# Attention layer of a hybrid decoder trunk: low parts of the weights and steps of the rotation move from GpSimd to VectorE

## The chip, the cores and the metric

The kernel runs on one core of a Trainium2 chip. A core has five engines with a queue of their own each: TensorE (PE in the profile, its weight loads PEld), VectorE (DVE), ScalarE (ACT), GpSimd (POOL) and SyncE (SP), which here issues all DMAs. Each engine takes its instructions in order and waits on semaphores for what others make. The metric is the device time of one execution in microseconds; less is better.

## The reference, cut to what matters

Two layers on a sequence of 1024 tokens with 1024 features: an attention layer with low-rank queries and keys (MLA), then a recurrent layer (RWKV-7). Each layer also attends to a memory of 256 tokens, gates with SiLU, and projects back. Only the first layer is touched by the change.

```
h = rmsnorm(x, norm_g[i]);  m = rmsnorm(mem, mem_norm_g[i])
mem_k, mem_v = split_cols(m @ w_mem_kv[i], (X_WIDTH, X_WIDTH))
u = h @ w_in_mla[j]
c_q, c_kv, k_rope_raw, q_mem, gate = split_cols(u, (384, 256, 64, 512, 2048))
q  = (rmsnorm(c_q, q_norm_g) @ w_uq).reshape(B, S, 12, 128 + 64)     # the last 64 rotated
kv = (rmsnorm(c_kv, kv_norm_g) @ w_ukv).reshape(B, S, 12, 128 + 128)
mix = causal softmax attention of 12 heads (block of 128 queries at a time)
mem_out = memory_attention(q_mem, mem_k, mem_v)
x = x + concatenate([mix, mem_out]) * silu(gate) @ w_out[i]

def apply_rope(x, cos, sin):
    x1, x2 = x[..., 0::2], x[..., 1::2]
    return stack([x1 * cos - x2 * sin, x1 * sin + x2 * cos])
```

## The kernel before

All matrices are kept transposed: features on the 128 partitions, 512 tokens (half of the sequence, `hf` 0 or 1) along the row. A float32 product is made of three matmuls in a narrower type: every operand is split into a high part, rounded (`wh`, `xh`), and a low part, the rest (`wl`, `xl`); `mm3` (lines 162 to 164) multiplies high by high, high by low and low by high. A high part is a cast on ScalarE, a low part a subtraction.

`weights` (line 142) fetches a block of weights in pieces of 512 columns: a DMA into one of four raw buffers `wr`, the cast on ScalarE (line 153), the subtraction (line 155). Four buffers each for `wh` and `wl` mean that a piece can be split only when PE has done with the one four pieces earlier. Which engine subtracts is decided in line 154: VectorE in the recurrent layer (`self.lows` is set there, line 941), GpSimd in the attention layer, and the two in turn for the memory's weights (`shared`).

The attention layer (`layer0`, line 414) runs in this order.

- `load_x` and `low` (about the first 100 us): the two halves of x are loaded and split (lines 440 and 441), and six column blocks of 128 are projected for either half (`mm_331` to `mm_986`, eight products of three matmuls each).
- The norms. `squares` (lines 182 to 186) squares on ScalarE and adds up on VectorE (`sqa`); `rstd_rows` sums over the partitions with a tiny matmul (line 208), then makes the reciprocal root in twelve small VectorE steps (lines 194 to 210) and spreads it (line 213); `rstd_spread` turns it with four transposes on PE (line 220). Five such chains stand in this stretch: x's first half (`b_289`, `b_309`), its second half (`b_581`, `b_601`), the two low-rank norms (`b_717`, `b_737` and `b_804`, `b_824`) and the memory (`b_1045`, `b_1063`). `tables` (lines 493 to 514) makes the rotation's sine and cosine, one half of the tokens at a time.
- `mem_load`, `mem_norm`, `mem_kv`: the memory is normed in four steps (`mn` line 255, `mh` and `ml` lines 128 and 129) and multiplied with the memory's weights (`mm_1271`, `mm_1309` and on).
- `mem_heads` and `gates`: the memory's attention and the gates, until about 450 us.
- `attend` and `project` (about 450 to 890 us): 48 tasks, 12 heads by four blocks of 256 queries, with the scores two tasks ahead of the values; in between `project` makes queries, keys and values of the head two further on. Every second head also makes the rotated queries of two heads: `rope` (line 516) multiplies by the cosine on VectorE (522), the swapped halves by the sine on GpSimd (523), and adds; lines 640 and 641 subtract for their low parts on GpSimd. GpSimd also clears two blocks of the transposed probabilities a task (line 730).
- `out_proj` of the first half, to about 965 us; that of the second half runs under the recurrent layer, with `self.lows` set.

No order is written out by hand between the engines. The generators interleave the pieces as the program is written, and a scheduler then orders the instructions of each engine from its own estimates of when what is ready; buffers are given out in the same pass. So where an instruction goes to another engine, the order on the others moves with it.

Of the kernel before, what the change touches and what calls it, by code (L numbers as in the profile page):

```python
# [13 lines left out]
F32 = mybir.dt.float32  # L14
# [57 lines left out]
class Build:  # L72
    def __init__(self, tc, A, st):
        self.tc, self.nc, self.A = tc, tc.nc, A
        self.n, self.lows = 0, False
        pool = lambda name, bufs, **kw: st.enter_context(tc.tile_pool(name=name, bufs=bufs, **kw))
        self.const = pool("const", 1)
        self.wp = pool("w", 4)
        self.w2p = pool("w2", 1)
        self.ws = pool("ws", 4)  # L80
        self.smp = pool("sm", 4)
        self.heap = pool("heap", 54)
        self.heap2 = pool("heap2", 12)
        self.mmp = pool("mmp", 2, space=PSUM)
        self.dram = pool("dram", 1, space=DRAM)
        self.ysp = [None, None]
        dt = lambda s: self.dram.tile([P, T], F32, tag=s, name=s)
        self.mkd = [[dt(f"mk{l}{i}") for i in range(2)] for l in range(2)]
        self.mvd = [[dt(f"mv{l}{i}") for i in range(2)] for l in range(2)]
        self.carry = [self.dram.tile([P, P], F32, tag=f"cr{p}", name=f"cr{p}") for p in range(NH)]  # L90
        self.setup()
# [47 lines left out]
        self.split(hi[:], lo[:], src)  # L139
        return hi, lo  # L140

    def weights(self, src, cols=1024, shared=False):


        nc = self.nc
        res = []
        for c in range(0, cols, T):
            n = min(T, cols - c)
            raw = self.wp.tile([P, T], F32, tag="wr", name=self.name("wr"))
            hi = self.ws.tile([P, T], F32R, tag="wh", name=self.name("wh"))  # L150
            lo = self.ws.tile([P, T], F32R, tag="wl", name=self.name("wl"))
            nc.sync.dma_start(raw[:, :n], src[:, c : c + n])
            nc.scalar.copy(hi[:, :n], raw[:, :n])  # L153
            sub = nc.vector.tensor_sub if self.lows or shared and len(res) % 2 else nc.gpsimd.tensor_sub
            sub(lo[:, :n], raw[:, :n], hi[:, :n].bitcast(F32))  # L155
            res.append((hi, lo))
        return res

# [104 lines left out]
    def mem_kv(self, l, ms):  # L263

        nc, A = self.nc, self.A
        mk, mv = [], []
        for h in range(4):
            if h % 2 == 0:
                mk.append(self.g([P, 2, 256], s="mk"))
            w = self.weights(A["wmk"][l, h], shared=True)  # L270
            ps = self.mmt()
            self.gemm(ps[:, :256], w, ms, 8)
            nc.scalar.copy(mk[-1][:, h % 2, :], ps[:, :256])
        for cb in range(2):
            ws = self.weights(A["wmv"][l, cb, 0], shared=True) + self.weights(A["wmv"][l, cb, 1], shared=True)
            ps = self.mmt()
            for mb in range(2):
                for k in range(8):
                    hi, lo = ws[k // 2]
                    o = (k % 2) * 256  # L280
                    m = tuple(x[:, mb * P : mb * P + P] for x in ms[k])
                    self.mm3(
                        ps[:, mb * 256 : mb * 256 + 256], m, (hi[:, o : o + 256], lo[:, o : o + 256]), k == 0, k == 7
                    )
            t = self.g(s="mv")
            nc.scalar.copy(t[:], ps[:])
            mv.append(t)
        for i, t in enumerate(mk):
            nc.sync.dma_start(self.mkd[l][i][:].rearrange("p (h m) -> p h m", h=2), t[:])
        for i, t in enumerate(mv):  # L290
            nc.sync.dma_start(self.mvd[l][i][:], t[:])
# [122 lines left out]
    def layer0(self, ahead):  # L414

        nc, A, tc = self.nc, self.A, self.tc
        with ExitStack() as st:
# [46 lines left out]
            raw = [[None] * 6 for _ in range(2)]  # L464
# [27 lines left out]
            cos, sin = tl([P, S], F32, "cos"), tl([P, S], F32, "sin")  # L492
# [23 lines left out]
            def rope(q, hf):  # L516

                sl = slice(hf * T, hf * T + T)
                sw, t = self.g(s="rs"), self.g(s="rt")
                for b in range(4):  # L520
                    nc.sync.dma_start(sw[32 * b : 32 * b + 32, :], q[32 * (b ^ 1) : 32 * (b ^ 1) + 32, :])
                nc.vector.tensor_mul(t[:], q[:], cos[:, sl])
                nc.gpsimd.tensor_mul(sw[:], sw[:], sin[:, sl])
                nc.vector.tensor_add(t[:], t[:], sw[:])
                return t

# [7 lines left out]
            def lows(hf):  # L534
                cq.append(lora(0, 3, PQG, hf, lambda s: tl([P, T], F32R, s)))
                yield
                ckv.append(lora(3, 2, PKVG, hf, lambda s: self.g(dt=F32R, s=s)))
                yield
                kr.append((tl([P, T], F32R, f"krh{hf}"), self.g(dt=F32R, s="krl")))
                self.split(kr[hf][0][:], kr[hf][1][:], rope(raw[hf][5], hf)[:])  # L540
                yield
# [66 lines left out]
            def project(h):  # L608
# [3 lines left out]
                if h % 2 == 0:  # L612
                    w = self.weights(A["wuq"][12 + hp], 384)
                    hd["qr"], heads[h + 1]["qr"] = [], []
                    for hf in range(2):
                        ps = self.mmt()
                        self.gemm(ps[:], w, cq[hf], 3)
                        q = self.g(s="rq")
                        nc.scalar.activation(q[:], ps[:], AF.Copy, scale=ATT_SCALE)
                        rot.append(rope(q, hf))  # L620
                        yield
                hd["qn"], hd["kn"] = [], []
                w = self.weights(A["wuq"][h], 384)
# [5 lines left out]
                w = self.weights(A["wkn"][h], 256)  # L629
# [5 lines left out]
                for t in rot:  # L635

                    a, b = self.g(dt=F32R, s="qsa"), self.g(dt=F32R, s="qsb")
                    nc.scalar.copy(a[0:64, :], t[0:64, :])
                    nc.scalar.copy(b[64:128, :], t[64:128, :])
                    nc.gpsimd.tensor_sub(a[64:128, :], t[0:64, :], a[0:64, :].bitcast(F32))  # L640
                    nc.gpsimd.tensor_sub(b[0:64, :], t[64:128, :], b[64:128, :].bitcast(F32))
                    hd["qr"].append(a)
                    heads[h + 1]["qr"].append(b)
                if h % 2 == 0:

                    w = self.weights(A["wv"][hp], 512)[0]
# [114 lines left out]
            for _ in project(0):  # L761
                pass
            for _ in project(1):
                pass
# [14 lines left out]
    def layer1(self, x1, first, second):  # L779

        nc, A, tc = self.nc, self.A, self.tc
        with ExitStack() as st:
# [155 lines left out]
                    next(gen, None)  # L938
                    yield

            self.lows = True
            N, now = 2 * NH, [0]
            stages = [(project, ST[0]), (lambda i: self.prep(items[i], env), ST[1]), (lambda i: self.invert(items[i], env), ST[2]), (scan, ST[3]), (norm, ST[4])]
            extra = {}
# [434 lines left out]
```

## Time and profile before

| | |
|---|---|
| median of 3 runs | 2541.62 us (2540.92 to 2550.03) |
| the profiled execution | 2544.33 us, its span 2542.6 us |
| TensorE busy | 2434.1 us, 96% |
| VectorE busy | 1883.6 us, 74% |
| ScalarE busy | 1371.9 us, 54% |
| GpSimd busy | 285.0 us, 11% |
| mean granted TensorE clock | 0.991 |

Most of GpSimd's time lies in the attention layer: 186.3 us for 148 weight subtractions. TensorE is the busiest engine in all stages but the first 128 us, so a stall of it is time lost and a stall of another engine usually is not. A wait is read at the instruction that waits, with its releaser behind the arrow.

### The profile page before, as it was taken

Reading aid. Unit: us, or ns where it says so; the run is one execution under the profiler, and the core shown is the slowest. Engines: PE = TensorE matmul, PEld = TensorE weight load, DVE = VectorE, ACT = ScalarE, POOL = GpSimd, SP = SyncE. Lnnn points to the kernel's source line nnn. Section 1 sums busy time; section 2 is a strip of 40 time slices with the busy share of each in tenths; the row PEclk is TensorE's granted clock in tenths of the full one; section 3 lists DMA queues with packets and bytes.
Section 4 is the critical chain, followed back from the end, with each engine's and each line's share of the span. In section 5 each row is a group of like instructions: output and inputs, shape, how many; then the busy total and the mean of one; then the engine's idle time right before and its main releaser. Section 6 shows DMA issues by size and latency. Waiting matters only on the chain.

```text
span 2542.6 us, 39928 instructions
## 1 busy us (share of the span) xinstructions
PE 2434.1 (96%) x13298; PEld 2003.9 (79%) x13298; DVE 1883.6 (74%) x5564; ACT 1371.9 (54%) x2971; POOL 285.0 (11%) x344
## 2 busy tenths in 40 slices
PE   7899999999999999999999999999999999999997
PEld 5688777888888787878777777877787777788885
DVE  6655433677777647679888888788888888786986
ACT  5444335555445434556566665666666665654542
POOL 3332222322222240000000000000000000000000
PEclk8899999999999999999999999999999999999998
DMA  4242222111111345331222222322222223232341
GB/s 155 88 157 96 91 83 80 50 50 60 55 54 56 135 140 178 122 106 61 80 67 70 74 83 82 120 76 76 69 78 74 75 80 102 92 105 97 115 141 69
DMA packets 165983, 231.46 MB, mean 91 GB/s; under 512 B 46096, under 2 KB 67984, under 8 KB 165776
## 3 DMA queue, kind: packets, MB, share of 16 engines
q1 hardware_dynamic: 165776, 228.90, 27.5%
q8 instruction: 105, 1.72, 0.3%
q14 instruction: 102, 0.84, 0.1%
HBM read 187.66 MB, written 37.49 MB: 89 GB/s over the span
## 4 chain that ended last, share of the span: by engine, by line
PE 69%; DVE 16%; ACT 6%; issue 3%; DMA 2%; SPq 0%; DVEq 0%; POOL 0%; ACTq 0%; POOLq 0%
PE mm L162 14%; PE mm L163 13%; PE mm L164 13%; PE a L1088 3%; DVE tmp L1139 2%; PE c L1221 2%; PE pt L726 2%; DVE U L1143 2%; PE c L1224 1%; PE po L162 1%; PE y L1228 1%; PE po L163 1%; DVE wl L155 1%; PE y L1227 1%; PE po L164 1%
## 5 line engine op out<-in xcount | busy, mean ns | idle before, releaser
L153 ACT CAST wh<-wr 128x512 fp32r<-128x512 f32 (+3 forms) x500 | 298.6, 599 | 461.6 <-PE mm L163 363.0
L162 PE MATMUL mm<-xnh,wh 128*128 128x512 f32 x912 | 374.1, 411 | 0.8 <-DVE qml L134 0.6
L163 PE MATMUL mm<-xnl,wh 128*128 128x512 f32 x912 | 371.4, 407 | 0.0
L164 PE MATMUL mm<-xnh,wl 128*128 128x512 f32 x912 | 369.8, 406 | 0.0
L155 DVE TENSOR_TENSOR wl<-wr,wh 128x512 fp32r<-128x512 f32 (+2 forms) x352 | 237.2, 676 | 98.7 <-ACT wh L153 79.8
L155 POOL TENSOR_TENSOR wl<-wr,wh 128x512 fp32r<-128x512 f32 (+1 forms) x148 | 186.3, 1263 | 579.4 <-ACT wh L153 446.0
L162 PE MATMUL mm<-yh,wh 128*128 128x512 f32 x492 | 199.8, 406 | 5.5 <-DVE xr L391 5.3
L164 PE MATMUL mm<-yh,wl 128*128 128x512 f32 x492 | 197.6, 402 | 0.0
L162 PEld LDWEIGHTS mm<-xnh,wh 128*128 128x128 f32 x912 | 172.2, 189 | 30.4 <-issue 2.6
L163 PE MATMUL mm<-yl,wh 128*128 128x512 f32 x492 | 196.1, 399 | 0.0
L163 PEld LDWEIGHTS mm<-xnl,wh 128*128 128x128 f32 x912 | 172.4, 189 | 27.2 <-issue 1.4
L164 PEld LDWEIGHTS mm<-xnh,wl 128*128 128x128 f32 x912 | 172.2, 189 | 27.2 <-issue 1.0
L1069 POOL MEMSET SAV<- 64x512 f32 x48 | 24.9, 524 | 1385.6 <-DVE m L1261 250.7
L162 PE MATMUL mm<-xh,wh 128*128 128x512 f32 x416 | 168.9, 406 | 7.2 <-ACT xh L440 7.2
L163 PE MATMUL mm<-xl,wh 128*128 128x512 f32 x416 | 168.6, 405 | 2.9 <-DVE xl L441 2.9
L164 PE MATMUL mm<-xh,wl 128*128 128x512 f32 x416 | 168.1, 404 | 0.0
L1139 DVE TENSOR_TENSOR tmp<-As,U 128x60 f32<-128x60 f32 (+24 forms) x744 | 156.8, 211 | 13.2 <-DMA U<-in_cst_dram 1.1
L1143 DVE TENSOR_TENSOR U<-U,tmp 128x60 f32<-128x60 f32 (+24 forms) x744 | 157.2, 211 | 11.9
L1235 ACT ACTIVATE sc<-S,f 128x128 f32<-128x128 f32 x168 | 67.4, 401 | 170.0 <-DVE S L1236 155.5
L304 ACT ACTIVATE p<-b,sm 128x512 f32<-128x512 f32 (+2 forms) x144 | 82.9, 579 | 117.2 <-DVE sm L301 78.0
L391 DVE TENSOR_TENSOR xr<-mm,xr 128x512 f32<-128x512 f32 x123 | 84.5, 689 | 77.7 <-PE mm L164 77.2
L162 PEld LDWEIGHTS mm<-yh,wh 128*128 128x128 f32 x492 | 93.1, 189 | 24.3 <-DVE xr L391 3.5
(362 smaller groups left out, 6214.3 us busy)
## 6 DMA issues: line engine op xcount, KB each, us to landing
wr<-in_wu_dram SPq DMA_DIRECT2D x292, 256.0 KB, 2.6
wr<-in_wo_dram SPq DMA_DIRECT2D x122, 256.0 KB, 2.6
yr<-y SPq DMA_DIRECT2D x60, 256.0 KB, 3.7
As<-sysd SPq DMA_DIRECT2D x24, 512.0 KB, 4.3
y<-y SPq DMA_DIRECT2D x32, 256.0 KB, 2.0
y<-sg SPq DMA_DIRECT2D x32, 256.0 KB, 2.0
g<-u SPq DMA_DIRECT2D x24, 256.0 KB, 2.4
gt<-g SPq DMA_DIRECT2D x24, 256.0 KB, 2.8
```

The source lines that it names most:

```text
L153: nc.scalar.copy(hi[:, :n], raw[:, :n])
L155: sub(lo[:, :n], raw[:, :n], hi[:, :n].bitcast(F32))
L162: mm(ps, a[0], b[0], start=start, stop=False)
L163: mm(ps, a[0], b[1], start=False, stop=False)
L164: mm(ps, a[1], b[0], start=False, stop=stop)
L304: nc.scalar.activation(p[:, :own], ps[:, :own], AF.Exp, bias=sm[:, 0:1], accum_out=sm[:, 2 + i : 3 + i])
L391: nc.vector.tensor_add(xs[m][:], ps[:], xs[m][:])
L726: nc.tensor.transpose(pt[:, o : o + P], src, self.ident)
L1088: mm(ps[:, j * 256 : j * 256 + 256], BK[c // 4][:, c % 4, :], AR[:, c, :], start=True, stop=True)
L1139: E.tensor_tensor(out=tmp[:, 0:u, 0:n], in0=As[:, 0:u, u : u + 1].broadcast_to([P, u, n]), in1=U[:, u : u + 1, i0:8].broadcast_to([P, u, n ...
L1143: E.tensor_tensor(out=U[:, 0:u, i0:8], in0=U[:, 0:u, i0:8], in1=tmp[:, 0:u, 0:n], op=ALU.add)
L1235: ACT.activation(sc[:], cur, AF.Copy, scale=fc)
```

## The change

Line 154 goes: every low part of a weight is subtracted on VectorE. In `rope` the product with the sine, and in `project` the two subtractions of the rotated queries' low parts, go to VectorE too. The argument `shared` and the switch `self.lows` go with it. What is computed is the same. GpSimd keeps its clearing of buffers and the mask.

```diff
-    def weights(self, src, cols=1024, shared=False):
+    def weights(self, src, cols=1024):
...
             nc.scalar.copy(hi[:, :n], raw[:, :n])
-            sub = nc.vector.tensor_sub if self.lows or shared and len(res) % 2 else nc.gpsimd.tensor_sub
-            sub(lo[:, :n], raw[:, :n], hi[:, :n].bitcast(F32))
+            nc.vector.tensor_sub(lo[:, :n], raw[:, :n], hi[:, :n].bitcast(F32))
...
                 nc.vector.tensor_mul(t[:], q[:], cos[:, sl])
-                nc.gpsimd.tensor_mul(sw[:], sw[:], sin[:, sl])
+                nc.vector.tensor_mul(sw[:], sw[:], sin[:, sl])
                 nc.vector.tensor_add(t[:], t[:], sw[:])
...
                     nc.scalar.copy(b[64:128, :], t[64:128, :])
-                    nc.gpsimd.tensor_sub(a[64:128, :], t[0:64, :], a[0:64, :].bitcast(F32))
-                    nc.gpsimd.tensor_sub(b[0:64, :], t[64:128, :], b[64:128, :].bitcast(F32))
+                    nc.vector.tensor_sub(a[64:128, :], t[0:64, :], a[0:64, :].bitcast(F32))
+                    nc.vector.tensor_sub(b[0:64, :], t[64:128, :], b[64:128, :].bitcast(F32))
...
-            self.lows = True
```

The diff doesn't show what the scheduler makes of it. Lines of the changed program are two or three lower. Three places follow.

VectorE, at the end of the first half of x and in the first norm chain, before: the low parts of x, then the additions of the squares (`sqa_265`), then the first small step behind the tiny matmul `b_289`.

```order
L441 SCALAR_TENSOR_TENSOR xl_254<-x_222,prm,xh_253 128x512
L441 SCALAR_TENSOR_TENSOR xl_258<-x_223,prm,xh_257 128x512
L441 SCALAR_TENSOR_TENSOR xl_262<-x_224,prm,xh_261 128x512
L992 TENSOR_TENSOR w2l_10937<-w_2387_10935,w2h_10936 128x256
L186 TENSOR_TENSOR sqa_265<-sqa_265,sqb_267 128x512
...
L186 TENSOR_TENSOR sqa_265<-sqa_265,sqb_282 128x512
L186 TENSOR_TENSOR sqa_265<-sqa_265,sqb_285 128x512
L210 TENSOR_SCALAR n_294<-b_289 128x8
```

And now:

```order
L439 SCALAR_TENSOR_TENSOR xl_254<-x_222,prm,xh_253 128x512
L153 TENSOR_TENSOR wl_367<-wr_365,wh_366 128x512
L439 SCALAR_TENSOR_TENSOR xl_258<-x_223,prm,xh_257 128x512
L153 TENSOR_TENSOR wl_420<-wr_418,wh_419 128x512
L439 SCALAR_TENSOR_TENSOR xl_262<-x_224,prm,xh_261 128x512
...
L184 TENSOR_TENSOR sqa_265<-sqa_265,sqb_282 128x512
L153 TENSOR_TENSOR wl_426<-wr_424,wh_425 128x512
L184 TENSOR_TENSOR sqa_265<-sqa_265,sqb_285 128x512
L153 TENSOR_TENSOR wl_474<-wr_472,wh_473 128x512
L208 TENSOR_SCALAR n_294<-b_289 128x8
```

The weights' low parts stand between the parts of x and between the links of the chain, one or two at a time.

TensorE, at the tiny matmul of the second norm chain (`b_581`, the second half of x), before: inside the last product of the first half, `mm_619`.

```order
L164 MATMUL mm_619<-xh_253,wl_615 128x512
L162 MATMUL mm_619<-xh_257,wh_614 128x512
L208 MATMUL b_581<-cst,sqa_409 128x2 x4
L163 MATMUL mm_619<-xl_258,wh_614 128x512
L164 MATMUL mm_619<-xh_257,wl_615 128x512
```

And now, inside the first product of the second half, `mm_681`:

```order
L161 MATMUL mm_681<-xl_459,wh_670 128x512
L162 MATMUL mm_681<-xh_458,wl_671 128x512
L206 MATMUL b_581<-cst,sqa_409 128x2 x4
L160 MATMUL mm_681<-xh_465,wh_670 128x512
L161 MATMUL mm_681<-xl_466,wh_670 128x512
```

It stands 14 rows further back (142 before, 156 now), with as many matmuls more ahead of it. The others of the five chains move the same way: `b_289` from row 49 to 52, `b_309` from 62 to 70, `b_601` from 157 to 179, `b_717` from 193 to 210, `b_737` from 219 to 253, `b_804` from 243 to 277, `b_824` from 260 to 298, `b_1045` from 336 to 375 and `b_1063` from 351 to 390.

TensorE, where the memory's first two heads of keys are made (`mm_1271` and `mm_1309`, from the parts `mh` and `ml` of the normed memory), before: 43 rows behind the norm's transpose `b_1063`, and one head after the other.

```order
L162 MATMUL mm_1271<-mh_1071,wh_1260 128x256
L163 MATMUL mm_1271<-ml_1072,wh_1260 128x256
L164 MATMUL mm_1271<-mh_1071,wl_1261 128x256
...
L162 MATMUL mm_1271<-mh_1078,wh_1260 128x256
L163 MATMUL mm_1271<-ml_1079,wh_1260 128x256
```

And now, four wide matmuls behind it, and the two heads side by side:

```order
L218 MATMUL b_1063<-cst,rw_1061 128x128 x2
L162 MATMUL mm_1227<-xh_566,wl_1196 128x512
L160 MATMUL mm_1227<-xh_573,wh_1195 128x512
L161 MATMUL mm_1227<-xl_574,wh_1195 128x512
L162 MATMUL mm_1227<-xh_573,wl_1196 128x512
L160 MATMUL mm_1271<-mh_1071,wh_1260 128x256
L160 MATMUL mm_1309<-mh_1071,wh_1298 128x256
L161 MATMUL mm_1271<-ml_1072,wh_1260 128x256
...
L161 MATMUL mm_1309<-ml_1072,wh_1298 128x256
...
L160 MATMUL mm_1271<-mh_1078,wh_1260 128x256
```

The norm's transpose has moved up against the products that need it. In the attention the scheduler moves pieces of neighbouring tasks by a few rows; behind the attention layer TensorE's order is the same.

## Rows read from the trace of the kernel before

**Rows 1.** The page's busy times: engine, us, share of span, instructions.

```profile
PE 2434.1 (96%) x13298; PEld 2003.9 (79%) x13298; DVE 1883.6 (74%) x5564; ACT 1371.9 (54%) x2971; POOL 285.0 (11%) x344
```

**Rows 2.** Stretches: length; busy us (instructions) by engine; granted clock, DMA share, GB/s.

```profile
0.00:128.00 128.00, 100.34 (x391) 78.67 (x392) 83.19 (x150) 58.96 (x104) 44.00 (x36) 0.89 0.36 120
450.00:890.00 440.00, 431.18 (x2700) 372.43 (x2700) 319.14 (x743) 221.83 (x546) 103.94 (x174) 1.00 0.21 66
1024.00:1088.00 64.00, 64.00 (x294) 52.61 (x293) 41.34 (x80) 33.46 (x60) 1.04 (x2) 1.00 0.36 122
1152.00:1216.00 64.00, 62.83 (x362) 50.96 (x361) 57.48 (x209) 37.00 (x87) 1.04 (x2) 1.00 0.22 68
```

**Rows 3.** TensorE's waits, first 128 us: total us, times, longest.

```profile
PE b L208 <- DVE sqa L186: 13.2, 4, 4.5
PE mm L162 <- ACT xh L440: 7.2, 1, 7.2
PE b L220 <- DVE rw L213: 4.3, 2, 3.1
PE mm L163 <- DVE xl L441: 2.9, 4, 0.8
```

**Rows 4.** Stretches at half clock: the first of five, and their sum.

```profile
28.50:35.20 6.70, 6.70 (x21) 5.44 (x21) 2.43 (x13) 0.26 (x1) 0.00 (x0) 0.50 0.85 265
...
sum 26.40, PE 23.01 PEld 18.91 DVE 13.66 ACT 5.64 POOL 2.69; mean PE 4.60 PEld 3.78 DVE 2.73 ACT 1.13 POOL 0.54
```

**Rows 5.** Timeline, TensorE at two chains: start, us, instruction, [idle before <-releaser].

```profile
28.24 1.72 PE L208 MATMUL b<-cst,sqa 128*128 128x2 f32 x8 [2.43 <-DVE sqa L186]
85.12 0.63 PE L220 MATMUL b<-cst,rw 128*128 128x128 f32 x4 [1.22 <-DVE rw L213]
```

**Rows 6.** Timeline, VectorE and GpSimd, first 50 us (equal neighbours merged).

```profile
9.93 2.75 DVE L441 SCALAR_TENSOR_TENSOR xl<-x,prm,xh 128x512 fp32r<-128x512 f32 x4 [1.12 <-ACT xh L440]
14.56 4.69 POOL L155 TENSOR_TENSOR wl<-wr,wh 128x512 fp32r<-128x512 f32 x3 [6.30 <-DMA wr<-in_wu_dram]
15.14 4.65 DVE L441 SCALAR_TENSOR_TENSOR xl<-x,prm,xh 128x512 fp32r<-128x512 f32 x3 [2.46 <-ACT xh L440]
20.05 8.13 DVE L186 TENSOR_TENSOR sqa<-sqa,sqb 128x512 f32<-128x512 f32 x7
32.41 0.43 DVE L213 COPY rw<-n 128x512 f32<-128x512 f32 x1
46.30 0.74 DVE L441 SCALAR_TENSOR_TENSOR xl<-x,prm,xh 128x512 fp32r<-128x512 f32 x1
47.56 0.68 DVE L186 TENSOR_TENSOR sqa<-sqa,sqb 128x512 f32<-128x512 f32 x1
48.16 1.79 DVE L441 SCALAR_TENSOR_TENSOR xl<-x,prm,xh 128x512 fp32r<-128x512 f32 x1
```

**Rows 7.** Groups, shapes apart: count, busy us, mean ns, idle before and releasers.

```profile
L155 DVE TENSOR_TENSOR wl<-wr,wh 128x512 fp32r<-128x512 f32 x334 | 231.5, 695 | 97.2 <-ACT wh L153 78.6 <-PE b L1151 9.8 <-PE c L1224 3.0
...
L155 POOL TENSOR_TENSOR wl<-wr,wh 128x512 fp32r<-128x512 f32 x118 | 158.5, 1349 | 399.5 <-ACT wh L153 345.8 <-PE mm L164 19.5 <-PE b L690 8.5
```

**Rows 8.** Timeline, VectorE: two tiny steps of a norm, two of a table.

```profile
30.20 0.17 DVE L194 TENSOR_SCALAR n<-n 128x8 int32<-128x8 int32 x1
30.41 0.17 DVE L195 TENSOR_SCALAR n<-n 128x8 int32<-128x8 int32 x1
...
151.33 0.42 DVE L507 TENSOR_SCALAR rn<-ang 128x512 f32<-128x512 f32 x1
151.79 0.69 DVE L508 SCALAR_TENSOR_TENSOR ang<-rn,ang 128x512 f32<-128x512 f32 x1
```

**Rows 9.** Timeline, the memory's norm: its arrival, its last low part.

```profile
129.17 0.37 ACT L222 COPY rstd<-b 128x256 f32<-128x256 f32 x1
...
137.82 1.01 DVE L129 TENSOR_TENSOR ml<-mn,mh 128x512 fp32r<-128x512 f32 x1 [0.69 <-ACT mh L128]
```

**Rows 10.** A full stretch of the attention, columns as in the second group.

```profile
540.00:549.00 9.00, 8.58 (x46) 6.55 (x45) 8.60 (x19) 3.90 (x11) 3.36 (x4) 1.00 0.25 73
```

More of the change, by code (lines that the diff above doesn't have):

```diff
@@ L74, in __init__ @@
         self.tc, self.nc, self.A = tc, tc.nc, A
-        self.n, self.lows = 0, False
+        self.n = 0
         pool = lambda name, bufs, **kw: st.enter_context(tc.tile_pool(name=name, bufs=bufs, **kw))
@@ L269, in mem_kv @@
                 mk.append(self.g([P, 2, 256], s="mk"))
-            w = self.weights(A["wmk"][l, h], shared=True)
+            w = self.weights(A["wmk"][l, h])
             ps = self.mmt()
@@ L274, in mem_kv @@
         for cb in range(2):
-            ws = self.weights(A["wmv"][l, cb, 0], shared=True) + self.weights(A["wmv"][l, cb, 1], shared=True)
+            ws = self.weights(A["wmv"][l, cb, 0]) + self.weights(A["wmv"][l, cb, 1])
             ps = self.mmt()
```

## The prediction, made before the change was run

> **What bounds the kernel now.** I read the page first: TensorE (PE) is busy 96% of the span, GpSimd (POOL) 11% [rows 1]. A change that touches nothing but the attention layer can therefore gain only where PE stands still, or is granted half its clock, before about 965 us, where that layer's weights end. The stretches say where that is [rows 2]: in the first 128 us PE is busy 100.3 us at a mean granted clock of 0.89; in the attention proper (450 to 890 us) 431.2 of 440, which leaves 9 us. So the first 128 us were read closely.
>
> There PE waits for VectorE (DVE) [rows 3]: 13.2 us at line 208 and 4.3 us at line 220, the two ends of the RMS-norm chain (squares added up on DVE, a small matmul, twelve tiny DVE steps, a transpose), and 2.9 us for the low parts of x. The other 7.2 us is the first load. Five stretches after such waits, the last until 127 us, show a granted clock of 0.50, that is 1.2 of 2.4 GHz (the first of them, and the sum of the five) [rows 4]. PE was busy 23.0 us in the five; at full clock that work takes half, so they cost 11.5 us. The shortest wait that has a half clock behind it is 2.43 us; one of 1.22 has none [rows 5].
>
> Why is DVE late? Four x low parts without POOL beside them start 0.67 us apart (2.75 us for four, the last lasting 0.74); three with POOL working take 4.65 us, 1.55 each, and POOL's own three take 4.69 [rows 6]. The chain's seven additions take 8.13 us, 1.16 each, with POOL beside most of them; one that POOL leaves alone gives way to the next after 0.60 (47.56 to 48.16). So a POOL subtraction doesn't run beside a DVE one that reads SBUF: each stretches the other.
>
> The Trainium skill (SBUF — State Buffer, "Who interferes with whom") says that a DVE instruction with two SBUF inputs contends with a GpSimd one that reads SBUF, and that whoever comes second waits for the whole of the other. The trace bears out the contention, with less than a whole turn: by the page three pairs would take about 3 x (1.28 + 0.67) = 5.9 us, an estimate; 4.65 was measured. By the page the first term below would be 1.2 us larger; I go by the row.
>
> **The change part by part.** *What leaves POOL.* Its rows in the program go from 349 to 163, so 186 instructions move: 118 weight subtractions of 128x512 at a mean of 1.35 us [rows 7], 30 narrower ones, 14 rotation products and 24 rotation subtractions. On DVE the same subtraction of 128x512 takes 0.695 us [rows 7]. All 186 at that price are 129 us, an upper bound. From below, DVE gets back what POOL held it up, in the first 128 us the difference between 1.55 or 1.16 and 0.6 to 0.67 for each stretched instruction. DVE is busy 83 of those 128 us with 30 instructions to come (POOL's 36 less six memsets and constants [rows 2]), 30 x 0.60 = 18 us. So DVE has room there, and the chain's own instructions get shorter.
>
> *The order.* The scheduler puts the low parts between the chain's links and moves the chain's PE instructions back: the ten of them stand 3, 8, 14, 22, 17, 34, 34, 38, 39 and 39 rows later in PE's order. At 0.23 us a wide matmul (64.00 us for 294 of all sizes, 0.22 [rows 2]) that is 0.7 to 9 us of other work ahead of each, where PE waited 1.2 to 4.5 us at six of them.
>
> *First term, x low parts.* In the new order DVE has, from 15.14 us on, three x parts and two weight parts, 5 x 0.65, and is done at 18.4; before, 15.14 + 4.65 = 19.8 [rows 6]. Gain 1.4 us.
>
> *Second term, the chain.* Waits of 17.5 us and 11.5 us of half clock are there to be had: 29.0 us.
>
> *Third term, what of it comes back.* Weight parts now stand in the chain on an in-order engine. The worst place is the third chain (b_717 to b_737): between its two PE instructions stand 42 matmuls, 9.7 us; DVE has there five weight parts and two products (7 x 0.60 = 4.2), four rotation-table steps of 0.42 and four of 0.69 (4.4), twelve tiny steps 0.20 apart (2.4) and a copy of 0.4 [rows 6, 8]: 11.4 us. So PE waits about 2 us there, where it waited 1.2. In the first chain a weight part (wl_528) must wait for a buffer that PE frees nine matmuls behind line 208; counted the same way PE waits 0.3. The other eight PE instructions give 0 to 0.7 each. Sum 4.6 us; bounds 1 (only the smallest stay) and 12 (each of the ten as long as the nearest row, 1.2). All are shorter than 2.4 us, so I price no half clock on them.
>
> *Fourth term, the memory norm.* This is a new wait. Before, the norm of the memory comes at 129.17 us and its last low part ends at 138.83, 9.7 us for four steps (multiply, cast on ScalarE, subtract) [rows 9], while PE still had 43 wide matmuls to do (9.9 us); its first memory matmul did not wait. Now the chain's end stands only four wide matmuls (0.9 us) ahead of the memory matmuls, and PE takes two heads' products side by side as the parts come. The four steps still take 9.7 us; three weight parts between them fill gaps that DVE has anyway, or add 0.4: 10.1. PE has 0.9 + 36 matmuls of half the width at 0.12 = 5.2 us of work in it. Loss 4.9 us (bounds 3 and 7). Half clock behind it, 3.4 us (a stretch like the first [rows 4]), is taken at an even chance, 1.7 us: the waits are small, but they come close together.
>
> *Fifth term, the rest, at nothing.* From 140 to 160 us PE waits for weight parts now and then; those parts will stand on DVE behind the second rotation table, which itself waits for a load. I count no change, bounds plus and minus 4. In the attention DVE is busy 319 of 440 us; POOL's 174 instructions there less 96 memsets that stay are 78 to come, at most 54 us: 373, 85%, before the stretching that goes. In a full stretch (540 to 549) DVE is busy 8.60 of 9.00 with two rotation products on POOL beside it [rows 10]. On DVE they are 1.2 us, more than the 0.4 left; if each stretched one DVE instruction by 0.9 (1.55 less 0.67), 1.8 us come back and 1.0 stays as cover. If not, PE loses 0.8 us in each of six such stretches, 5 us. The output projection has the same loop in the next layer with its weights on DVE already: PE busy 64.0 of 64.0 us [rows 2]. Behind 965 us PE keeps its order and only moves forward.
>
> **Sum.** 1.4 + 29.0 - 4.6 - 4.9 - 1.7 = 19.2 us. The profiled execution took 2544.3 us (span 2542.6 and 1.7 around it); the median of the runs is 2541.6, 2.7 below it. I take the gain off the median: 2541.6 - 19.2 = 2522.4, say 2522.
>
> **Rivals.** *All of it comes (2509).* The third term goes to 1, the fourth to nothing, the half clock stays away, and 3 of the attention's 9 us come too: 1.4 + 29.0 - 1 + 3 = 32.4. For it: without POOL beside it DVE has the lengths that its rows show when alone. Against: the memory norm's four steps are plain arithmetic.
>
> *It is handed back (2536).* An in-order DVE holds the chain behind weight parts that wait for PE's buffers: the third term is 12, the fourth 7, the second table costs 4, the half clock 1.7; 30.4 - 24.7 leaves 5.7 us. For it: weight parts stand between the links of every chain. Against: counted through, a buffer decides at three places, by 0.3 us each.
>
> *DVE becomes the bound in the attention (2556).* There are 48 tasks of 256 queries, each with a chain of maximum, exponential, reciprocal and product across DVE and ScalarE, begun two tasks ahead. If one moved instruction of 0.7 us stands in front of it in every task and PE is out of other work, 48 x 0.7 = 34 us are lost against 19 won: 15 us slower. It decides from 0.4 us a task on. For it: 8.6 of 9 us. Against: half of the moved ones come in lumps, at every second head, and in the next layer DVE is busy 57.5 of 64 us while PE is at 62.8 [rows 2].
>
> The Trainium skill (Perfetto Trace Analysis, "Optimizing Scalar/DVE Operations") speaks for this rival: with DVE saturated, giving work to GpSimd may pay. The same place adds that the two share an SBUF read port, so that it may not. The rows show DVE at 73% with the stretching in it, which is not saturated.
>
> **How the numbers follow.** A gain of 12 to 28 us as reckoned: 0.60. All of it: 0.12. Handed back: 0.20. Bound in the attention: 0.08. A measurement of this kernel can tell about 0.5%, 12.7 us, from no change; the first two give faster 0.72, the third same 0.20, the last slower 0.08. The range goes from 2510 (all of it but 1 us) to 2540, past the handed-back case; it leaves out about 0.15.
>
> **What would show it.** Right: PE busy at least 108 us of the first 128; waits at lines 206 and 218 (208 and 220 before) under 7 us; at most two stretches at 0.50 before 130 us; PE waiting 3 to 7 us in small pieces for the memory norm's parts; the attention within 3 us of its old length; the next layer unchanged. Wrong: waits of more than 2 us at three or more of the chains; PE waiting for weight parts over 8 us; or PE below 97% in the attention with a product of the softmax on DVE as releaser.

## The result and the profile after

The changed kernel takes 2514.65 us in the median (2510.56 to 2517.97, 6 runs), the kernel before 2542.05 (2539.20 to 2550.03, 6 runs): 27.4 us less, which is 0.9892 of the one median over the other; over all runs the ratio is 0.9887, with a 95% interval of 0.9871 to 0.9904. The forecast was 2522, a gain of 19.2 us. The direction and the place were right; the size was too small by 8 us.

The profiled execution of after is its fastest (2510.56 us, span 2508.8), that of before is 2.3 us above its median. So the two traces are 33.8 us apart, 6.4 more than the medians. The busy times of the page after (beside [rows 1]):

```profile
PE 2420.2 (96%) x13298; PEld 1996.1 (80%) x13298; DVE 1936.4 (77%) x5750; ACT 1375.7 (55%) x2973; POOL 55.1 (2%) x158
```

VectorE has 186 instructions more and is busy only 52.8 us longer; TensorE has the same work and is busy 13.9 us less. Of that 11.9 us is work no longer done at half clock: at a granted clock of 0.50 it was busy 31.7 us before and 7.9 after, over the whole span. The other 2 us were not traced. By stretches (columns as in [rows 2]):

```profile
0.00:128.00 128.00, 110.19 (x503) 87.26 (x504) 94.27 (x209) 68.77 (x121) 0.71 (x6) 1.00 0.43 145
...
450.00:890.00 440.00, 432.59 (x2690) 375.85 (x2690) 337.20 (x791) 219.65 (x530) 28.32 (x98) 1.00 0.22 73
```

TensorE gets through 503 matmuls in the first 128 us, where it got through 391. Its waits there (total us, times, longest), to be held against [rows 3]:

```profile
PE mm L160 <- ACT xh L438: 7.6, 2, 7.0
PE mm L160 <- ACT mk L271: 3.2, 1, 3.2
PE b L218 <- DVE rw L211: 2.0, 3, 1.3
PE mm L160 <- ACT mh L128: 1.6, 2, 1.1
PE mm L161 <- DVE ml L129: 1.4, 4, 0.6
PE b L206 <- DVE sqa L184: 1.2, 1, 1.2
PE mm L161 <- DVE xl L439: 0.6, 2, 0.3
```

The two ends of the norm chains are waited for 3.2 us in all, where it was 17.5. Of the five stretches at a granted clock of 0.50 [rows 4] none is left behind a chain; one has come behind the new wait for `mk`:

```profile
126.98:130.39 3.41, 3.41 (x18) 3.41 (x17) 3.03 (x6) 1.34 (x3) 0.00 (x0) 0.50 0.08 31
```

Two marks divide the rest of the program: TensorE's first score product (`b<-knh`) and its first product of the output projection (`mm<-yh`). Their rows in the timelines (start, us, instruction), before and then after:

```profile
441.46 0.28 PE L683 MATMUL b<-knh,qnh 128*128 128x256 f32 x1
...
838.49 0.40 PE L162 MATMUL mm<-yh,wh 128*128 128x512 f32 x1
```

```profile
413.46 0.28 PE L681 MATMUL b<-knh,qnh 128*128 128x256 f32 x1
...
807.01 0.40 PE L160 MATMUL mm<-yh,wh 128*128 128x512 f32 x1
```

The table has the start of the first, the time from the first to the second, and the span.

| trace | first score product | attention to the projection | span |
|---|---|---|---|
| before | 441.46 | 397.0 | 2542.6 |
| after | 413.46 | 393.6 | 2508.8 |
| e1, weights only | 414.43 | 397.4 | 2516.5 |
| e2, rotation only | 437.19 | 393.6 | 2536.5 |
| e3, opening only | 413.59 | 397.2 | 2527.2 |
| e12, attention only | 436.00 | 393.5 | 2534.3 |

28.0 of the 33.8 us are won before the attention, 3.4 in it, the other 2.4 behind it. Each line is a single execution.

### The profile page after: what moved, and what is told of

Same layout as the page of the kernel before. It is cut to its first block, busy times and chain, and to the rows that moved or that the text cites. A ratio compares the mean times of both kernels' runs of the same rounds, so it can differ in the third digit from the quotient of the medians.

```text
span 2508.8 us, 39875 instructions
## 1 busy us (share of the span) xinstructions
PE 2420.2 (96%) x13298; PEld 1996.1 (80%) x13298; DVE 1936.4 (77%) x5750; ACT 1375.7 (55%) x2973; POOL 55.1 (2%) x158
## 4 chain that ended last, share of the span: by engine, by line
PE 75%; DVE 15%; ACT 6%; issue 3%; DMA 2%; SPq 0%; DVEq 0%; ACTq 0%
PE mm L160 15%; PE mm L161 15%; PE mm L162 15%; PE a L1085 3%; PE c L1218 2%; DVE tmp L1136 2%; PE pt L724 2%; DVE U L1140 2%; PE c L1221 1%; PE y L1225 1%; PE po L160 1%; PE po L161 1%; PE y L1224 1%; DVE wl L153 1%; PE po L162 1%
## 5 line engine op out<-in xcount | busy, mean ns | idle before, releaser
L153 DVE TENSOR_TENSOR wl<-wr,wh 128x512 fp32r<-128x512 f32 (+3 forms) x500 | 329.6, 661 | 132.3 <-ACT wh L152 113.0
L297 DVE TENSOR_REDUCE sm<-b 128x1 f32<-128x256 f32 (+1 forms) x176 | 90.3, 527 | 24.8 <-PE b L686 10.1
L162 PEld LDWEIGHTS mm<-yh,wl 128*128 128x128 f32 x492 | 92.7, 188 | 17.0 <-issue 0.2
```

The lines of the kernel that those rows point to most:

```text
L153: nc.vector.tensor_sub(lo[:, :n], raw[:, :n], hi[:, :n].bitcast(F32))
L162: mm(ps, a[1], b[0], start=False, stop=stop)
L297: nc.vector.tensor_reduce(sm[:, i : i + 1], ps[:, :own], AX.X, ALU.max, negate=True)
```

## The experiments

The theory: GpSimd's subtractions read SBUF and stretch VectorE's; the norm chains are therefore late, TensorE waits for them and then works at half clock. The rival: what covers the chains is the new order, whoever subtracts. Times are beside the kernel before on the same chip.

| run | median us | before | ratio | 95% interval |
|---|---|---|---|---|
| e1, weights only | 2520.06 | 2545.84 | 0.9896 | 0.9872 to 0.9919 |
| e2, rotation only | 2538.61 | 2545.84 | 0.9973 | 0.9962 to 0.9983 |
| e3, opening only | 2523.98 | 2545.84 | 0.9915 | 0.9891 to 0.9938 |
| e4, shadow | 2551.46 | 2545.84 | 1.0020 | 1.0008 to 1.0033 |
| e5, positions early | 2518.55 | 2546.77 | 0.9890 | 0.9875 to 0.9905 |
| e6, memory norm early | 2514.38 | 2546.77 | 0.9873 | 0.9859 to 0.9888 |
| e7, clears beside | 2520.77 | 2546.77 | 0.9899 | 0.9884 to 0.9914 |
| e8, before without reads | 2513.59 | 2546.77 | 0.9865 | 0.9848 to 0.9882 |
| e9, positions first | 2516.91 | 2545.10 | 0.9888 | 0.9871 to 0.9906 |
| e10, memory early, keys first | 2516.23 | 2545.10 | 0.9891 | 0.9875 to 0.9907 |
| e11, the change again | 2517.69 | 2545.10 | 0.9896 | 0.9881 to 0.9912 |
| e12, attention only | 2536.08 | 2545.52 | 0.9956 | 0.9938 to 0.9973 |

### GpSimd's reads, or the order: e4 and e8

e4 puts GpSimd's reads back and leaves the changed order alone (`shade` is set in the attention layer only):

```diff
             nc.vector.tensor_sub(lo[:, :n], raw[:, :n], hi[:, :n].bitcast(F32))
+            if self.shade is not None:
+                nc.gpsimd.tensor_sub(self.shade[:, :n], hi[:, :n].bitcast(F32), hi[:, :n].bitcast(F32))
```

> The changed kernel, and for every weight piece of the attention layer a subtraction on GpSimd that reads the same high part and writes a buffer that nobody reads. VectorE, ScalarE and TensorE keep the changed kernel's order up to the end of the attention; only GpSimd's reads of SBUF come back (on all pieces, 164 in place of 148). Theory A (GpSimd's reads stretch VectorE, and that makes the chains late): VectorE's additions of squares go back from 0.6 to over 1.0 us where GpSimd works, chain waits of 8 us or more and two or more stretches at half clock in the first 130 us, 2528 to 2545 us. Theory B (the new order covers the chains, whoever subtracts): chain waits under 5 us, at most one stretch, within 6 us of the changed kernel, 2511 to 2521 us.

e8 is the opposite: the order before, but GpSimd reads nothing for a weight and clears the buffer, so that the low part is left out:

```diff
-            sub = nc.vector.tensor_sub if self.lows or shared and len(res) % 2 else nc.gpsimd.tensor_sub
-            sub(lo[:, :n], raw[:, :n], hi[:, :n].bitcast(F32))
+            if self.lows or shared and len(res) % 2:
+                nc.vector.tensor_sub(lo[:, :n], raw[:, :n], hi[:, :n].bitcast(F32))
+            else:
+                nc.gpsimd.memset(lo[:, :n].bitcast(F32), 0.0)
```

> The kernel before, but each subtraction of a weight's low part on GpSimd is a clear of the same buffer (the low part is left out, and nothing of SBUF is read for it); VectorE's share of work stays what it was, and TensorE's order moves by a few rows only, in eight places. Rotation steps stay on GpSimd. Theory A (the stretching makes the chains late): additions of squares back at 0.7 us, waits at lines 208 and 220 in the first 128 us 6 us or less (17.5 before), ratio to the kernel before 0.985 to 0.992, with the old order. Theory B (the order that the scheduler now chooses is what covers the chains): waits of 10 us or more stay, ratio 0.994 or more.

VectorE's additions of squares and low parts of x in the first 160 us, shapes apart (count, busy us, mean ns, idle before). Before:

```profile
L186 DVE TENSOR_TENSOR sqa<-sqa,sqb 128x512 f32<-128x512 f32 x17 | 18.1, 1063 | 1.1 <-ACT sqb L185 0.4
L441 DVE SCALAR_TENSOR_TENSOR xl<-x,prm,xh 128x512 fp32r<-128x512 f32 x16 | 15.9, 1024 | 7.4 <-ACT xh L440 7.4
```

After:

```profile
L439 DVE SCALAR_TENSOR_TENSOR xl<-x,prm,xh 128x512 fp32r<-128x512 f32 x16 | 11.7, 749 | 2.3 <-ACT xh L438 2.2
L184 DVE TENSOR_TENSOR sqa<-sqa,sqb 128x512 f32<-128x512 f32 x17 | 11.7, 688 | 0.5
```

e4, and its weight parts, which take 0.688 us in the changed kernel:

```profile
L153 DVE TENSOR_TENSOR wl<-wr,wh 128x512 fp32r<-128x512 f32 x41 | 38.2, 933 | 11.2 <-ACT wh L152 10.9 <-issue 0.4
L442 DVE SCALAR_TENSOR_TENSOR xl<-x,prm,xh 128x512 fp32r<-128x512 f32 x16 | 16.7, 1067 | 0.2 <-ACT xh L441 0.2
L186 DVE TENSOR_TENSOR sqa<-sqa,sqb 128x512 f32<-128x512 f32 x17 | 14.0, 821 | 0.5
```

e8:

```profile
L443 DVE SCALAR_TENSOR_TENSOR xl<-x,prm,xh 128x512 fp32r<-128x512 f32 x16 | 11.8, 751 | 9.3 <-ACT xh L442 9.3
L188 DVE TENSOR_TENSOR sqa<-sqa,sqb 128x512 f32<-128x512 f32 x17 | 11.7, 689 | 2.6 <-ACT sqb L187 1.9
```

TensorE's waits for the chains in the first 160 us, e4 first, then e8:

```profile
PE b L220 <- DVE rw L213: 6.9, 5, 2.2
PE b L208 <- DVE sqa L186: 6.6, 3, 2.6
```

```profile
PE b L210 <- DVE sqa L188: 3.4, 2, 2.9
PE b L222 <- DVE rw L215: 1.6, 3, 1.0
```

With the new order and GpSimd's reads the chains cost 13.5 us of waiting again, and the kernel is slower than before; at 2551 us it is 6 us above what the theory gave, and why it is slower still than the kernel before was not traced. With the old order and no reads they cost 5.0 and the whole gain is there, 33 us in the median. So the order is not what wins the time; the reads are what cost it. The order even costs some: the waits for `mk`, `mh` and `ml` that the changed kernel has (3.2, 1.6 and 1.4 us) are absent from e8. The additions in e4 came to 0.82, not over 1.0 us as expected: there the low parts of x (1.07) and the weight parts (0.93) carry most of the stretch.

A rival that no run separates: e4 and e8 also change when GpSimd gives buffers back. In the first 160 us ScalarE's casts of weights (`wh`) wait for GpSimd 6.6 us before, 7.6 in e4 and not at all in e8, where the clears don't wait for the load and the cast either. The rows speak against it for the chains: in the kernel before, VectorE sits idle for 1.1 us in all ahead of the 17 additions, 0.4 of it for ScalarE's squares, while each addition takes 1.06 us in place of 0.69. So it is the length of the additions that the chain shows, not operands that come late.

### Which of the moved steps: e1, e2, e3, e12

e1 changes line 154 alone, e2 lines 523, 640 and 641 alone. e3 sets `self.lows` from the start and takes it back ahead of the first head; e12 sets it there and has e2's three lines too.

> Only the weights' low parts go to VectorE; the rotation's product and the two subtractions of rotated queries stay on GpSimd. Theory (the gain comes from the opening, where only weights stand in TensorE's way): nearly all of the 27 us, 2514 to 2519 us; waits at the norm chains of the first 128 us under 6 us. Rival (the rotation steps in the attention carry a part of it): 2520 to 2530 us.

> Only the rotation's product and the two subtractions go to VectorE; all weights as in the kernel before. Theory (opening): no gain to speak of, 2538 to 2543 us; the five stretches at half clock before 130 us are still there. Rival (attention): 2530 to 2536 us. If VectorE were the bound in the attention: above 2545 us.

> The weights' low parts go to VectorE up to the start of the attention proper (about 450 us) only; from there on, and for all rotation steps, GpSimd as before. Theory (opening): 2515 to 2521 us, the opening as in the changed kernel, the attention as before. Rival (the attention's 38 freed subtractions and the output projection's count as well): 2522 to 2530 us.

> The counterpart of the run with the opening alone: the weights' low parts go to VectorE from the start of the attention proper on, and all rotation steps do (two of fourteen products lie in the opening); the weights of the opening stay with GpSimd. Theory (VectorE has room in the attention and GpSimd's reads cost a little there too): 5 to 10 us faster than the kernel before, ratio 0.996 to 0.998, the five stretches at half clock of the opening still there. Rival (VectorE becomes the bound in the attention): ratio 1.003 or more. If the parts don't add up (the opening alone gave 0.9915, the whole change 0.989): ratio 1.000.

e1's theory was missed: 2520.06 us is 1 us above its range and at the foot of its rival's (2520 to 2530). Its chain waits, 2.7 us, are under the 6 that were expected. e3 gives 21.9 of the change's 27.4 us, so most comes from the opening; its median, too, lies in its rival's range (2522 to 2530), and the rest counts as well. e2 took 2538.61 us, in its theory's range, but the kernel before ran at 2545.84 beside it: a gain of 7.2 us where 0 to 3 were expected.

The table of marks tells where a part of it lies: the attention is 3.4 us shorter where the rotation steps have left GpSimd (after, e2, e12) and as long as before in e1 and e3, where they haven't, with the attention's weights on either engine. Two runs lie between, so something of the weights counts there as well, though what was not traced: e8, with the rotation on GpSimd and nothing read for weights, at 394.9 us, and e4, with the rotation on VectorE and the reads for weights back, at 395.0. In the opening e2 is 4.3 us ahead and e12, which moves the same steps there, 5.5: their chain waits in the first 128 us are 14.6 and 15.9 us where they were 17.5, and the rest was not traced (two executions of the changed kernel differ there by 2.3 us, 413.46 and 415.72).

VectorE has not become the bound: e12, with all of the attention's moved steps, is 9.4 us faster. e3 and e12 together gain 31.3 us, 3.9 more than the change; their intervals allow it.

In the attention the rotation steps on GpSimd stretched the softmax's products and the rotation's own product with the cosine. The groups of e1, where they are still there (414.43 to 811.83 us), and of e2, where they are gone (437.19 to 830.78 us):

```profile
L309 DVE TENSOR_SCALAR p<-p,sm 128x512 f32<-128x512 f32 x66 | 40.2, 623 | 1.8
...
L522 DVE TENSOR_TENSOR rt<-rq,cos 128x512 f32<-128x512 f32 x10 | 9.1, 908 | 0.0
```

```profile
L309 DVE TENSOR_SCALAR p<-p,sm 128x512 f32<-128x512 f32 x66 | 31.9, 498 | 1.8
...
L522 DVE TENSOR_TENSOR rt<-rq,cos 128x512 f32<-128x512 f32 x10 | 6.8, 683 | 0.8 <-ACT rq L619 0.8
```

How these lengths become 3.4 us of TensorE is not shown. From before to after TensorE's idle time between the two marks falls by 1.4 us (5.2 to 3.9); the other 2.1 us is shorter busy time for the same matmuls, at a granted clock of 1.00 in both.

### GpSimd's clears: e7

Two clears of an unused buffer on GpSimd for each weight piece, 115 us of them in the first 128, nothing else changed.

> The changed kernel, and GpSimd clears a buffer that nobody reads, two clears for each weight piece, back to back from the start to about 210 us. All other engines keep the changed kernel's order exactly. Theory A2 (it is GpSimd's reading of SBUF that stretches VectorE): additions of squares stay at 0.69 us, within 4 us of the changed kernel, ratio to the kernel before 0.986 to 0.990. Theory A1 (any work of GpSimd on SBUF stretches VectorE): additions over 0.9 us in the opening, ratio 0.993 or more.

The additions stay at 0.689 us and the ratio is within the range of A2. The waits for the chains still rise, from 3.2 to 6.6 us; the section on the hardware says which instructions have a part in it.

### The wait for mk: e5, e6, e9, e10

In the changed kernel TensorE waits 3.2 us for ScalarE's copy of the memory's keys. The timeline (start, us, instruction, [idle before <-releaser]):

```profile
120.41 1.10 SPq L493 DMA_DIRECT2D pos<-in_pos_dram  x1
...
124.55 0.43 DVE L495 CAST ang<-pos 128x512 f32<-128x512 int32 x1 [0.97 <-DMA pos<-in_pos_dram]
...
125.06 0.65 ACT L271 COPY mk<-mm 128x256 f32<-128x256 f32 x2 [2.20 <-DVE ang L495]
...
125.48 0.38 PE L160 MATMUL mm<-mh,wh 128*128 128x256 f32 x1 [3.21 <-ACT mk L271]
```

The copy waits for the cast that reads the positions, and the cast for their load. e5 (cut to one place) puts the load ahead of the memory's:

```diff
...
             def memory():
+                pi = positions(1)
                 mem.extend(self.mem_load(b_tile))
                 ms.append(self.mem_norm(0, *mem))
                 yield
-                tables(1)
+                tables(1, pi)
```

> The changed kernel, with the load of the second half's token positions (for the second rotation table) put ahead of the memory's loads; else the same work, TensorE's order the same but for the memory norm's two small matmuls, which stand 4 and 5 rows further back. It is about TensorE's wait of 3.2 us near 125 us for ScalarE's copy of the memory's keys (mk). Theory (that copy gets the buffer in which the positions lie and waits for VectorE to have read them, which waits for their late load): the wait goes, and the half-clock stretch behind it; 3 to 5 us less than the changed kernel, ratio to the kernel before 0.984 to 0.988. Rival (the products behind it then wait for the memory's weights, which arrive late too): 0 to 1 us, ratio 0.987 to 0.991.

The wait fell to 0.9 us, and the memory came late instead (ScalarE's first square, then TensorE's waits):

```profile
104.62 0.42 ACT L180 ACTIVATE sqa<-memr 128x256 f32<-128x256 f32 x1 [4.03 <-DMA memr<-in_memT_dram]
```

```profile
PE mm L160 <- ACT mh L128: 3.2, 2, 2.7
PE b L206 <- DVE sqa L184: 3.0, 1, 3.0
```

e9 loads both halves' positions one behind the other, well ahead of the memory.

> The changed kernel, with the second half's positions loaded right behind the first half's, some 30 us ahead of the memory's loads; TensorE and ScalarE keep the changed kernel's order row for row, VectorE has a few steps of the second table earlier. The run with the load put directly ahead of the memory's loads only moved the wait: the memory arrived later. Theory (the late positions are the whole of the 3.2 us wait for mk, and their place directly ahead of the memory was what brought the new one): the wait for mk falls under 1 us, the memory's chain keeps its 1.2 us or less, the half-clock stretch behind goes; 3 to 5 us less than the changed kernel in the same chip's runs. Rival (the memory's weights, behind the same loads, are next late): within 2 us of the changed kernel.

The wait for `mk` is 0.9 us again, so its cause is the late load, as the theory has it. The memory's first square came within 1 us of its old place, its chain still cost 1.7 us (1.2 before), and another chain 1.2. The time, 2516.91, is 0.8 us under the changed kernel's beside it: no gain that can be told, where 3 to 5 us were expected.

e6 and e10 bring the memory's norm forward, both with the positions early too, e10 with the rotation of the keys ahead of the second low-rank norm.

> As the run with the positions early, and the memory's load and norm written side by side with the low-rank norms, so that the norm's transpose stands about 80 matmuls ahead of the products that need it, not directly ahead. Theory (the fourth step of the prediction: the normed parts are late because the norm stands close in front of its products): the 3.0 us of waits for mh and ml go as well, ratio to the kernel before 0.982 to 0.987. Rival (the second low-rank chain, now moved back, is waited for in their place): no better than the run with the positions early.

> As the run with the memory's norm early, with both position loads first, and the rotation of the keys ahead of the second low-rank norm. In that run ScalarE's copy of mk stood behind the cast krh on ScalarE's in-order queue, which waited for the rotation, and TensorE waited 6.1 us. Theory: krh comes earlier, the 6.1 us goes, the waits for mh and ml stay away: 4 to 8 us less than the changed kernel in the same chip's runs, ratio to the kernel before 0.984 to 0.987. Rival (the second low-rank norm, now last, holds ScalarE in the same way): within 2 us of the changed kernel.

In both the waits for `mh` and `ml` are gone. In e6 the copy of `mk` then stood behind a cast that waited for the rotated keys, in e10 the last low-rank chain was held up, and TensorE waited another 3.1 us, for `mk`. The row of ScalarE in e6, and TensorE's wait:

```profile
125.14 0.62 ACT L128 CAST krh<-rt 128x512 fp32r<-128x512 f32 x1 [4.65 <-DVE rt L525]
```

```profile
PE mm L160 <- ACT mk L271: 6.1, 1, 6.1
```

In e10, VectorE between two of the twelve tiny steps, and the end of that chain:

```profile
113.67 0.17 DVE L192 TENSOR_SCALAR n<-n 128x8 int32<-128x8 int32 x1
113.74 0.68 DVE L153 TENSOR_TENSOR wl<-wr,wh 128x512 fp32r<-128x512 f32 x1
...
114.95 0.17 DVE L193 TENSOR_SCALAR n<-n 128x8 int32<-128x8 int32 x1
...
121.81 1.08 PE L218 MATMUL b<-cst,rw 128*128 128x128 f32 x4 [5.87 <-DVE rw L211]
```

The tiny steps, 0.20 us apart elsewhere, took from 112.99 to 121.20 us, since weight parts and table steps stand between them. Neither kernel can be told from the change (e6 0.9873, e10 0.9891, the change 0.9887 and 0.9896). In time, e5, e9 and e10 came out in the ranges of their rivals, and e6 just above its theory's (0.982 to 0.987). I have no version that clearly beats the change.

### The change again: e11

> The changed kernel itself, on the chip of the two runs beside it, to compare them with: ratio to the kernel before 0.987 to 0.991, as before.

The median was 2517.69, and this profile 10.3 us longer than the first. Its opening has two stretches at half clock where the first had one, and two lie near 835 and 944 us, where the first had none. TensorE was busy 16.3 us in the four and 3.4 in the one, so half of 12.9, 6.5 us, is clock; the rest was not traced. The longest:

```profile
834.96:841.79 6.83, 6.08 (x25) 5.83 (x26) 2.95 (x6) 0.64 (x2) 0.00 (x0) 0.50 0.52 170
```

It begins in a wait of 4.6 us that ends at 835.7; the same wait is 2.7 us in the first profile, with no half clock behind it. The first of the four stands behind the end of a chain, at a wait of 1.98 us:

```profile
107.18 0.58 PE L206 MATMUL b<-cst,sqa 128*128 128x2 f32 x4 [1.98 <-DVE sqa L184]
```

```profile
107.92:111.33 3.41, 3.41 (x9) 2.65 (x8) 2.43 (x13) 0.62 (x1) 0.00 (x0) 0.50 0.20 77
```

So some stretches come in one execution and not in the other, and differences of some 5 us between two single profiles prove nothing here. The attention's length does stand apart: 393.4 us in this profile, 393.4 to 393.6 in e5, e6, e7, e9 and e10.

## Why the prediction was right, and where it was short

*What bounds the kernel*: right. The gain lies where TensorE stood still before the attention.

*The price on VectorE*: right. A moved subtraction takes 0.685 us (0.695 said), and VectorE's additions and low parts of x fall back to 0.69 and 0.75 us. That this, not the order, is the cause the prediction only argued; e4, e7 and e8 show it. The order's rows, on which I spent a paragraph, decide little of the chains' gain; what the order did bring are the new waits of the fourth term and for `mk`, which e8, with the old order, has not got.

The terms are held against the two traces, 33.8 us apart, as they were worked out from one of them.

*First term, 1.4 us*: the waits for `xl` fell from 2.9 to 0.6, those for `xh` rose from 7.2 to 7.6: a gain of 1.9.

*Second and third, 29.0 less 4.6*: 17.5 us of waits became 3.2, and the half clock behind them, 11.5 us, is gone: 25.8 where 24.4 was said. The worst place was named rightly, the end of the third chain, a wait of 1.27 us at 75.11, where 2 was reckoned. That no half clock stands behind the chains is in part luck: the prediction put none on waits under 2.4 us, but e11, the same kernel, has one behind 1.98 us, and e9 one behind 1.70.

*Fourth, 4.9 and 1.7 us*: the waits for the memory norm's parts came, 1.6 and 1.4, so 3.0 in all. A half clock of 1.7 us came (3.41 us of busy TensorE), but behind `mk`.

*Fifth, the rest at nothing*: this is the step that failed. It is 10.0 of the 14.6 us that the two traces have beyond the sum of 19.2, and so most of what the forecast lacks; for the weight parts alone bounds of 4 had been given, and their 3.6 lies within. Five things stood in it. Against the change the wait for `mk`, 3.0 us more than before: I had named the table and its load, but not that TensorE would come to the copy before the load lands. For it, the waits from 145 us to the attention, of which before had these and some smaller:

```profile
PE pt L336 <- DVE mp L309: 2.5, 3, 0.9
PE mm L164 <- DVE wl L155: 1.5, 2, 1.0
PE mm L163 <- POOL wl L155: 1.1, 1, 1.1
PE mm L163 <- DVE wl L155: 1.0, 1, 1.0
```

and after only this:

```profile
PE mm L160 <- DVE qnl L134: 0.6, 1, 0.6
```

The parts' 3.6 us went, and 3.6 of the others, most of them in the memory's attention, whose softmax VectorE does under GpSimd's reads too (`mp`, 128x256: a mean of 0.453 us before, 0.350 after). To these come 3.4 us in the attention (the rotation, by e2 and e12), and 2.4 behind it, of which 1.7 are a half clock at 970 us (TensorE busy 3.41 us), which the first profile of after hasn't got. That is -3.0 + 3.6 + 3.6 + 3.4 + 2.4 = 10.0. With 1.9 + 25.8 - 3.0 - 1.7 the sum is 33.0 of the traces' 33.8. I had counted the stretching only where TensorE waited longest, though the same rows hold it wherever VectorE reads SBUF beside GpSimd.

*Profile and median*: I took the gain off the median. The profiled execution of after is 4.1 us under its median, that of before 2.3 above its own. Stretches that come in some executions only (e11) can do that; that they did it here is not shown. So some of what the traces gain, the 1.7 us at 970 us for one, may be the executions' and not the change's.

*The rivals.* All of it comes (2509): of its parts the third term came near (3.2 against 1), the attention's 3 us did come, the memory norm's waits stayed; the measured time lies halfway between it and the forecast. Handed back (2536): not in the change. e10 shows something near it at one chain, 5.87 us and a half clock: the chain's tiny steps stand between weight parts and table steps in VectorE's order, though VectorE is busy 8.1 of those 8.2 us and doesn't wait for PE's buffers, as the rival has it. Bound in the attention (2556): fell; e12 is faster.

*What was to be seen*: TensorE busy 110.2 of 128 us (108 said), chain waits 3.2 (under 7), one stretch (two at most), the memory norm's parts 3.0 (3 to 7). The attention was 3.4 us shorter, just out of the 3 said.

## What to carry to other kernels

Moving two-operand work from an idle GpSimd to a busier VectorE can pay: what GpSimd reads from SBUF at the same time lengthens VectorE's instructions, so look at one VectorE instruction's duration with GpSimd beside it and without, and multiply by all of them, not only by those on the chain that waits longest. A busy share of VectorE that is measured under such reads overstates its load: 186 instructions came here for 52.8 us. When a wait goes, look for the next in-order queue behind it: a load put directly ahead of others moved the wait to them, and put further ahead it took the wait away without a gain that could be told.

## What the runs showed of the hardware

GpSimd's clears read nothing and leave VectorE's two-operand instructions alone (0.689 us), but lengthen most of those with one operand from SBUF. Two small steps and two table steps in the first 128 us, after:

```profile
L497 DVE TENSOR_SCALAR rn<-ang 128x512 f32<-128x512 f32 x2 | 0.9, 426 | 0.1
...
L192 DVE TENSOR_SCALAR n<-n 128x8 int32<-128x8 int32 x4 | 0.7, 165 | 0.0
```

and e7, where these lines stand three and four lower, with two groups that keep their lengths:

```profile
L195 DVE TENSOR_SCALAR n<-n 128x8 int32<-128x8 int32 x4 | 1.6, 410 | 0.0
...
L501 DVE TENSOR_SCALAR rn<-ang 128x512 f32<-128x512 f32 x1 | 0.7, 709 | 0.0
...
L211 DVE TENSOR_SCALAR n<-b 128x8 f32<-128x8 f32 x4 | 0.7, 167 | 2.3 <-PE b L209 2.3
...
L214 DVE COPY rw<-n 128x512 f32<-128x512 f32 x4 | 1.7, 424 | 0.1
```

The small step from SBUF takes 0.410 us beside clears of 0.54 us and 0.165 without, the table step 0.709 and 0.426; the one from PSUM (`n<-b`) takes 0.167 in both, and the four copies that spread a chain's result (`rw<-n`) take 0.424 and 0.423. Why the copies are spared is not shown. Two such small steps from SBUF in each chain add some 0.5 us to it, which is a part of the 3.4 us by which e7's chain waits rose; the rest wasn't traced.

The Trainium skill (SBUF — State Buffer, "Who interferes with whom") has both halves of this: two inputs from SBUF contend with a GpSimd instruction that reads, not with one that only writes, while copies, casts and single-tensor steps in their two-port modes contend with GpSimd at all. The rows of e4, e7 and e8 agree; in which mode a step of e7 ran they don't show. That the second comes to a full stop until the first is done, as the prediction takes from that page, the rows don't show: pairs took 1.55 us [rows 6], less than 0.67 and 1.28 together, the lengths that the prediction takes for either alone.
